# Routing over 32 masked logits, a gather of its own for the first pair of experts, and the last pair's gate and up products put ahead of the down product in front of it

## The chip, the cores and the metric

One NeuronCore of a Trainium2 chip runs the whole program in one launch. The metric is the device time of an execution in microseconds (us); the time before is the median of three runs, 1452.24 us (1451.04 to 1452.6). Matrix work runs on TensorE (PE), element-wise work on VectorE (DVE), ScalarE (ACT) and GpSimd (POOL); SyncE (SP) issues the transfers from the chip's memory (HBM).

## The reference, cut to what matters

Two transformer layers with a dense feed-forward part are followed by one block with two kinds of attention and a mixture of experts (MoE), and a last norm. 256 tokens of width 1024; 32 experts in 4 groups of 8; two experts a token, both from the token's best group. The part that the change touches:

```python
def hier_moe(h, w_group, b_group, w_router, b_router, w_e_gate, w_e_up, w_e_down):
    g_logits = hf @ w_group + b_group                       # 256 x 4
    g_probs, g_top = softmax(g_logits), argmax(g_logits)
    g_w = g_probs[g_top]
    e_logits = (hf @ w_router + b_router).reshape(-1, 4, 8)[:, g_top]   # 256 x 8
    e_w, e_idx = lax.top_k(softmax(e_logits), 2)
    e_w = e_w / e_w.sum()
    gates = one_hot(g_top * 8 + e_idx, 32) weighted by g_w * e_w        # 256 x 32
    for e in range(32):                                     # 1024 -> 512 -> 1024
        a = silu(hf @ w_e_gate[e]) * (hf @ w_e_up[e])
        out = out + gates[:, e:e+1] * (a @ w_e_down[e])
    return out

x = x + hier_moe(rmsnorm(x, g_ffn), ...)
return rmsnorm(x, g_final)
```

All arithmetic is in float32. The weights of the experts are 32 x 3 matrices of 2 MB, some 200 MB in all.

## The kernel before, in words

All weights come through one stream (`Stream`, lines 154 to 231): a list of units, most of them of 1 MB, in the order in which they are used, loaded by SP into slots of SBUF. `pump` issues the next unit as soon as a slot is free, `free` gives a slot back when the matmuls that read it have been written down. The slots come from tiles named raw, raw_left, raw_right, arena and arena_y, so a transfer into any of these from in_w_e_gate, in_w_e_up or in_w_e_down is a unit of the experts.

Up to the MoE a planner sets the order of the side work. From `route` on the order of each engine is the order of the code.

`route` (line 1955) makes the choice on DVE from the logits `lg` (two halves of 128 tokens, 4 group and 32 expert logits each). `top` finds the first maximum of a row as a one-hot: a maximum, a comparison, a product with a falling ramp, a maximum, a comparison. It runs on the 4 groups, then, after the 8 logits of the chosen group have been picked out with a product and a sum, twice on 8 logits. The one-hot of both experts is spread to 32 columns (`s32`), and two matmuls count the tokens in front of each token (`place`: which of an expert's CAP = 32 places it has). While DVE does this, PE runs WARM matmuls whose result nobody reads (`ident` by `x`, 512 columns; PE takes each float32 matmul in two passes, and the profile counts passes).

`side_batch` (line 2130) readies 8 experts (4 pairs) at a time: `places` writes the one-hot of token and place for them (2 x 256 columns, tile arena_y), `rows(k2)`, for k2 = 0 to 3, gathers the tokens into `xe` with 4 matmuls of 128 x 256 (two of the 8 blocks of the width), `scales` gathers the norm's factors, and two steps `back` make the gated transpose that scatters the results. These steps stand in a list (`todo`), from which `side` takes one or two between the steps of a pair.

`moe` (line 2309) goes through 16 pairs of experts (NQ). A pair q takes `emit_rows(q, 0)` and `emit_rows(q, 1)` (gate and up products; each reads 4 units of 1 MB, 16 matmuls, four at a time in four strips of 32 columns of PE's array: two experts, gate and up), `emit_act` (tanh on ACT, two steps on DVE), `emit_at` (four transposes and an ACT copy) and `emit_down` (4 units of 1 MB). After each second pair `emit_scatter` adds the results into four banks of PSUM, which also take `x`.

The order of the stream is pair by pair: 8 units of gate and up, 4 of down. The last pair's down comes in 8 units of 0.5 MB (`last_down`), the first four for output columns 0 to 511, the others for 512 to 1023. `last_norm` (line 2362) takes the last pair's down product in these two halves: matmuls, a copy of the 64 rows to SBUF (`Y`), two scatter matmuls, and for each 128 tokens a square with a sum (ACT) and the product with `g_final` (DVE). Then POOL makes the factor of the norm, ACT and DVE scale, and four transfers of 256 KB write the output. A branch (`If self.most > CAP`), for the case that an expert gets over 32 tokens, stands inside the last pair; it is not entered.

Of the kernel before, what the change touches and what calls it, by code (L numbers as in the profile page):

```python
# [13 lines left out]
P = 128  # L14
T = 256
D = 1024
# [34 lines left out]
WARM = 5  # L51
# [519 lines left out]
class Kernel:  # L571
# [992 lines left out]
    def plan2(self):  # L1564
# [32 lines left out]
        def last_down(q):  # L1597

            for c in range(2):
                for h in range(2):  # L1600
                    for e in (2 * q, 2 * q + 1):
                        src = self.A["w_e_down_2"][0][e][h * 256 : h * 256 + 256, c * 512 : c * 512 + 512]
                        self.exp_units[q].append(
                            self.st.add(512, 2, [(0, 512, src.rearrange("(p k) c -> p k c", p=P))], split=False)
                        )

        for q in range(NQ):
            rows(q)
            (down if q < NQ - 1 else last_down)(q)
# [250 lines left out]
    def mix2(self):  # L1860
# [44 lines left out]
        self.gp = self.small([P, 2, 4], "gp", bufs=1)  # L1905
        for h in range(2):
# [48 lines left out]
    def route(self):  # L1955
# [22 lines left out]
        def top(v, n, oh):  # L1978

            m = sc(f"top{n}{oh}", 1)  # L1980
            o = sc(f"oh{n}{oh}", n)
            t = sc(f"tt{n}", n)
            V.tensor_reduce(out=m, in_=v, axis=AX.X, op=ALU.max)
            V.tensor_tensor(out=t, in0=v, in1=bc(m, 2, n), op=ALU.is_equal)
            V.tensor_tensor(
                out=t, in0=t, in1=bc(self.tab(f"first{n}").unsqueeze(1), 2, n), op=ALU.mult
            )
            f = sc(f"tf{n}", 1)
# [5 lines left out]
        gm, go = top(gl, 4, "a")  # L1994
        el, e48 = sc("el", 8), sc("e48", 4, 8)
        V.tensor_tensor(
            out=e48,
            in0=lg[:, :, 4:36].rearrange("p t (g e) -> p t g e", g=4),
            in1=bc(go.unsqueeze(3), 2, 4, 8),
            op=ALU.mult,  # L2000
        )
        V.tensor_reduce(out=el, in_=e48.rearrange("p t g e -> p t e g"), axis=AX.X, op=ALU.add)
        m1, o1 = top(el, 8, "a")
        e2 = sc("e2", 8)
        V.scalar_tensor_tensor(out=e2, in0=o1, scalar=-BIG, in1=el, op0=ALU.mult, op1=ALU.add)
        m2, o2 = top(e2, 8, "b")
        s32, sel = sc("s32", 4, 8), sc("sel", 8)

        def spread(out, v):
            V.tensor_tensor(out=out, in0=bc(go.unsqueeze(3), 2, 4, 8), in1=bc(v.unsqueeze(2), 2, 4, 8), op=ALU.mult)  # L2010

        V.tensor_tensor(out=sel, in0=o1, in1=o2, op=ALU.add)
        spread(s32, sel)
        s32 = s32.rearrange("p t g e -> p t (g e)")
# [11 lines left out]
        self.gate = sc("g32", 4, 8)  # L2026

        def gates():
            den = sc("den", 1)
            V.tensor_reduce(out=gs, in_=ge, axis=AX.X, op=ALU.add)  # L2030
            V.scalar_tensor_tensor(out=den, in0=v, scalar=1.0, in1=gs, op0=ALU.add, op1=ALU.mult)
            V.reciprocal(out=den, in_=den)
            V.tensor_tensor(out=o2, in0=o2, in1=bc(v, 2, 8), op=ALU.mult)
            V.tensor_tensor(out=o1, in0=o1, in1=o2, op=ALU.add)
            V.tensor_tensor(out=o1, in0=o1, in1=bc(den, 2, 8), op=ALU.mult)
            spread(self.gate, o1)
            self.gate = self.gate.rearrange("p t g e -> p t (g e)")
# [92 lines left out]
    def side_batch(self, b):  # L2130
# [6 lines left out]
        def places():  # L2137
            for tb in range(2):
                nc.vector.tensor_tensor(
                    out=d[:, tb].rearrange("p (e s) -> p e s", e=8),  # L2140
                    in0=self.place[:, tb, e0 : e0 + 8].unsqueeze(2).to_broadcast([P, 8, CAP]),
                    in1=self.tab("iota").unsqueeze(1).to_broadcast([P, 8, CAP]),
                    op=ALU.is_equal,
                )
            self.xe[b] = self.room(NK, 8 * CAP)

        def rows(k2):
# [3 lines left out]
            for i in range(2):  # L2151
                k = k2 * 2 + i
                for tb in range(2):

                    c0 = (k // 4) * 512
                    self.mm(ps[:, i, :], self.x[:, tb, c0 + k % 4 : c0 + 512 : 4], d[:, tb, :], tb == 0, tb == 1)
            gain = lambda k: self.gp[:, k // 4, k % 4 : k % 4 + 1]
            k = k2 * 2
            nc.scalar.activation(out=xe[:, k, :], in_=ps[:, 0, :], func=AF.Copy, scale=gain(k))
            nc.vector.tensor_scalar(out=xe[:, k + 1, :], in0=ps[:, 1, :], scalar1=gain(k + 1), scalar2=None, op0=ALU.mult)  # L2160
# [35 lines left out]
        steps = [places] + [lambda k2=k2: rows(k2) for k2 in range(4)] + [scales]  # L2196
# [73 lines left out]
    def emit_at(self, th):  # L2270

        ps = self.ps(5)[:, 0:256]
        for k in range(4):

            c0 = (k // 2) * 256
            self.tr(ps[:, k * 64 : k * 64 + 64], th[0:64, c0 + k % 2 : c0 + 256 : 2])
# [32 lines left out]
    def moe(self):  # L2309
# [14 lines left out]
        for q in range(NQ):  # L2324
# [7 lines left out]
            if q == NQ - 1:  # L2332
                side(99)
# [3 lines left out]
            if q == NQ - 1:  # L2337
                with self.tc.If(self.most > CAP):
                    self.overflow()
                self.gfin = self.room(D)  # L2340
                nc.gpsimd.dma_start(out=self.gfin, in_=self.A["g_final_2"].unsqueeze(0).to_broadcast([P, D]))
# [11 lines left out]
            if q == NQ - 1:  # L2353
                break
# [5 lines left out]
        self.last_norm(at)  # L2360

    def last_norm(self, at):
# [3 lines left out]
        outs = [[self.room(512) for tb in range(2)] for c in range(2)]  # L2366
        for c in range(2):
            self.emit_down(NQ - 1, at, c)
            self.emit_scatter(NQ // 2 - 1, c)
            for tb in range(2):  # L2370
                ps = self.ps(c * 2 + tb)
                nc.scalar.activation(
                    out=self.ps(7), in_=ps, func=AF.Square, scale=D ** -0.5, accum_out=self.ssq[:, tb, c : c + 1]
                )
                V.tensor_tensor(out=outs[c][tb], in0=ps, in1=self.gfin[:, c * 512 : c * 512 + 512], op=ALU.mult)
        v = self.small([P, 2], "v")
        nc.gpsimd.tensor_tensor(out=v, in0=self.ssq[:, :, 0], in1=self.ssq[:, :, 1], op=ALU.add)
        nc.gpsimd.tensor_scalar(out=v, in0=v, scalar1=EPS, scalar2=None, op0=ALU.add)
        self.pow(self.rstd, v)
        for c in range(2):  # L2380
            for tb in range(2):
                o, r = outs[c][tb], self.rstd[:, tb : tb + 1]
                if c + tb == 0:
# [3 lines left out]
                (nc.sync if c else nc.scalar).dma_start(  # L2387
# [282 lines left out]
```

## Time and profile before

| | |
|---|---|
| median of 3 runs | 1452.24 us (1451.04 to 1452.6) |
| profiled execution | 1452.91 us, its span 1451.1 us |
| PE busy | 1311.3 us (90%), 8865 passes |
| DVE, ACT, POOL busy | 724.6, 559.8, 215.9 us |
| transfers | 360.21 MB, mean 248 GB/s |
| granted PE clock, mean | 0.953 of full |

The span is the time from the first to the last instruction that the profiler recorded. A row of a timeline has the start, the time taken, the engine and the line, the operation, what it writes and reads, and the shape. Line 258 is that of a helper that issues every instruction, so rows are told apart by their tiles. PE is the matmul itself, PEld the loading of its stationary operand, SPq the issue of a transfer on SP's queue. A matmul's row holds its way through the array too, so matmuls that follow each other overlap in the rows. In a row of windows the busy time and the count of each engine stand in the order PE, PEld, DVE, ACT, POOL, then the granted PE clock (1.00 is 2.4 GHz, 0.50 is 1.2 GHz), the busy share of the 16 transfer engines and what they moved.

### The profile page before, as it was taken

The numbers are of one execution on the slowest core, as the hardware profiler recorded it, in microseconds if no ns is written. First come the engines' busy times: TensorE is split into PE (matmuls) and PEld (weight loads), VectorE is DVE, ScalarE is ACT, GpSimd is POOL, SyncE is SP. The second block draws the span as 40 slices with busy tenths as digits, with TensorE's granted clock in tenths as the row PEclk, the third lists the DMA queues.
The fourth block names the chain that finished last, engine by engine and source line by source line (L and its number), as shares of the span: only waits on it lengthen the run. The fifth ranks groups of instructions, "written<-read, shape, count | busy, mean of one in ns | idle before, by whom it ended". The sixth has DMA issues, their size and how long they took to land.

```text
span 1451.1 us, 23004 instructions
## 1 busy us (share of the span) xinstructions
PE 1311.3 (90%) x8865; PEld 977.9 (67%) x8865; DVE 724.6 (50%) x1521; ACT 559.8 (39%) x1175; POOL 215.9 (15%) x345
## 2 busy tenths in 40 slices
PE   9989999999999999999999999998887777867665
PEld 8777999988777899988989899885332311412111
DVE  5586677765588677765676655563210200110001
ACT  5526555554536555545564546541110100100001
POOL 2154111101055011102442302010000000000000
PEclk9998999999999999999999999999989979988888
DMA  9651556555524465557435354688999999999995
GB/s 342 193 170 47 162 179 199 167 195 177 178 96 147 131 189 183 186 188 225 152 94 169 117 163 141 220 327 354 419 420 420 421 421 420 420 421 421 421 419 211
DMA packets 155076, 360.21 MB, mean 248 GB/s; under 512 B 8752, under 2 KB 98352, under 8 KB 130768
## 3 DMA queue, kind: packets, MB, share of 16 engines
q1 hardware_dynamic: 152928, 354.81, 66.8%
q0 software_dynamic: 1248, 3.11, 0.7%
q8 instruction: 71, 1.16, 0.3%
q10 hardware_dynamic: 784, 0.76, 0.2%
q14 instruction: 45, 0.37, 0.1%
HBM read 357.60 MB, written 1.05 MB: 247 GB/s over the span
## 4 chain that ended last, share of the span: by engine, by line
PE 41%; DMA 22%; DVE 3%; ACT 2%; POOL 1%; issue 1%; POOLq 0%; DVEq 0%; SPq 0%; ACTq 0%
PE psum L258 41%; DMA raw<-in_w_e_up_dram 8%; DMA raw_left<-in_w_e_down_dram 3%; DMA arena_y<-in_w_e_up_dram 3%; DMA raw<-in_w_e_down_dram 3%; DMA raw_right<-in_w_e_up_dram 3%; DMA raw_right<-in_w_e_down_dram 1%; DMA raw_left<-in_w_e_up_dram 1%; DVE arena L258 1%; ACT whi L258 1%; ACT arena L258 1%; DVE wlo L258 1%; POOL arena L258 1%; DVE arena_o L258 0%; ACT arena_o L258 0%
## 5 line engine op out<-in xcount | busy, mean ns | idle before, releaser
L258 DVE TENSOR_TENSOR wlo<-raw,whi 128x512 fp32r<-128x512 f32 (+3 forms) x552 | 397.2, 727 | 260.5 <-ACT whi L258 249.4
L258 ACT CAST whi<-raw 128x512 fp32r<-128x512 f32 (+3 forms) x552 | 332.8, 606 | 344.6 <-PE psum L258 274.4
L258 PE MATMUL psum<-h_hi,whi 128*128 128x256 f32 x1040 | 297.8, 286 | 3.0 <-ACT whi L258 3.0
L258 PE MATMUL psum<-h_lo,whi 128*128 128x256 f32 x1040 | 291.6, 280 | 0.1
L258 PE MATMUL psum<-h_hi,wlo 128*128 128x256 f32 x1040 | 290.2, 279 | 0.0
L258 PEld LDWEIGHTS psum<-h_hi,whi 128*128 128x128 f32 x1040 | 195.8, 188 | 10.1 <-issue 4.8
L258 PEld LDWEIGHTS psum<-h_lo,whi 128*128 128x128 f32 x1040 | 196.2, 189 | 0.9 <-issue 0.5
L258 PEld LDWEIGHTS psum<-h_hi,wlo 128*128 128x128 f32 x1040 | 196.0, 188 | 0.2 <-DVE wlo L258 0.2
L258 PE MATMUL psum<-raw,arena 128*32 128x512 f32 x608 | 164.0, 672 | 19.1 <-DMA raw<-in_w_e_up_dram 12.6
L258 PE MATMUL psum<-arena 64*128 64x128 f32 (+10 forms) x752 | 160.1, 418 | 21.6 <-DVE arena L258 8.2
L258 PE MATMUL psum<-whi,h_hi 128*128 128x256 f32 (+3 forms) x448 | 145.8, 325 | 1.4 <-ACT arena_o L258 1.1
L258 PE MATMUL psum<-whi,h_lo 128*128 128x256 f32 (+3 forms) x448 | 138.3, 309 | 0.0
L258 PE MATMUL psum<-wlo,h_hi 128*128 128x256 f32 (+3 forms) x448 | 138.3, 309 | 0.0
L258 PEld LDWEIGHTS psum<-arena 64*128 64x128 f32 (+4 forms) x752 | 73.1, 175 | 69.8 <-issue 23.7
L258 DVE SCALAR_TENSOR_TENSOR arena<-arena,psum 128x256 f32<-128x256 f32 (+2 forms) x36 | 17.8, 517 | 201.7 <-ACT arena L258 198.8
L258 PEld LDWEIGHTS psum<-raw,arena 128*32 128x32 f32 x608 | 34.4, 121 | 99.8 <-issue 60.3
L258 PE MATMUL psum<-raw_left,arena 128*32 128x512 f32 x400 | 81.2, 712 | 20.9 <-DMA raw_left<-in_w_e_gate_dram 14.8
L258 POOL TENSOR_TENSOR arena<-arena 128x512 f32<-128x512 f32 (+2 forms) x46 | 49.0, 1074 | 295.3 <-DVE arena L258 289.0
L258 PEld LDWEIGHTS psum<-whi,h_hi 128*128 128x128 f32 x448 | 85.3, 190 | 11.0 <-issue 4.4
L258 PEld LDWEIGHTS psum<-wlo,h_hi 128*128 128x128 f32 x448 | 85.4, 191 | 4.6 <-issue 1.4
L258 PEld LDWEIGHTS psum<-whi,h_lo 128*128 128x128 f32 x448 | 85.2, 190 | 4.5 <-DVE h_lo L258 0.2
L258 DVE COPY arena<-psum 128x384 f32<-128x384 f32 (+6 forms) x60 | 32.6, 543 | 108.0 <-ACT arena L258 95.7
(247 smaller groups left out, 1761.5 us busy)
## 6 DMA issues: line engine op xcount, KB each, us to landing
raw<-in_w_e_up_dram SPq DMA_DIRECT2D x32, 1024.0 KB, 19.8
raw<-in_w_in_dram SPq DMA_DIRECT2D x60, 512.0 KB, 4.9
raw<-in_w_e_gate_dram SPq DMA_DIRECT2D x24, 1024.0 KB, 19.8
raw<-in_w_gate_dram SPq DMA_DIRECT2D x44, 512.0 KB, 4.0
raw<-in_w_up_dram SPq DMA_DIRECT2D x44, 512.0 KB, 5.1
raw<-in_w_down_dram SPq DMA_DIRECT2D x20, 1024.0 KB, 5.2
raw_left<-in_w_e_gate_dram SPq DMA_DIRECT2D x20, 1024.0 KB, 19.9
raw<-in_w_e_down_dram SPq DMA_DIRECT2D x19, 1024.0 KB, 19.8
```

The costliest lines, as they stand in the source:

```text
L258: return f(*args, **kw)
```

## The change

**Routing.** The three parts of `el` go: instead of the product, the sum over the groups and a choice among 8, the logits of the other groups get -BIG (`top(..., others=True)` gives the one-hot of those that are not the first maximum), and both choices are made on 32 columns, with a ramp `first` of 32 that POOL writes in `mix2`. Two spreads from 8 to 32 columns go too. The one-hots and the scratch lie in a room of the arena that `gates` drops. WARM goes from 5 to 3.

**First pair.** For the first 8 experts, `places` and `rows` take columns c0 to c1: first those of pair 0 alone (64 columns), later, after the pair's second half, those of pairs 1 to 3 (192 columns).

**Last pair.** The stream takes the gate and up units of pair 15 ahead of the down units of pair 14, and `moe` does the same with `emit_rows` and `emit_act`; the branch and the load of `g_final` stand behind them. The last down comes in 512, 256 and 256 output columns, one unit an expert and piece, and `last_norm` has one round for each.

```diff
-WARM = 5
+WARM = 3
...
-            for c in range(2):
-                for h in range(2):
-                    for e in (2 * q, 2 * q + 1):
...
+            for c0, n in ((0, 512), (512, 256), (768, 256)):
+                for e in (2 * q, 2 * q + 1):
+                    src = self.A["w_e_down_2"][0][e][:, c0 : c0 + n].rearrange("(p k) c -> p k c", p=P)
+                    self.exp_units[q].append(self.st.add(n, 4, [(0, n, src)], split=False))
...
+        for q in range(NQ - 1):
             rows(q)
-            (down if q < NQ - 1 else last_down)(q)
+            if q == NQ - 2:
+                rows(NQ - 1)
+            down(q)
+        last_down(NQ - 1)
...
-            V.tensor_tensor(out=o, in0=t, in1=bc(f, 2, n), op=ALU.is_equal)
+            V.tensor_tensor(out=o, in0=t, in1=bc(f, 2, n), op=ALU.is_lt if others else ALU.is_equal)
...
-        V.tensor_reduce(out=el, in_=e48.rearrange("p t g e -> p t e g"), axis=AX.X, op=ALU.add)
-        m1, o1 = top(el, 8, "a")
...
+        V.scalar_tensor_tensor(
+            out=el.rearrange("p t (g e) -> p t g e", g=4),
+            in0=bc(no.unsqueeze(3), 2, 4, 8),
+            scalar=-BIG,
+            in1=lg[:, :, 4:36].rearrange("p t (g e) -> p t g e", g=4),
+            op0=ALU.mult,
+            op1=ALU.add,
         )
+        m1, _ = top(el, self.first, 32, "a", (o1, t))
+        V.scalar_tensor_tensor(out=e2, in0=o1, scalar=-2.0 * BIG, in1=el, op0=ALU.mult, op1=ALU.add)
+        m2, _ = top(e2, self.first, 32, "b", (o2, t))
+        V.tensor_tensor(out=s32, in0=o1, in1=o2, op=ALU.add)
...
+            one, rest = slice(0, 2 * CAP), slice(2 * CAP, 8 * CAP)
+            steps = [lambda: places(0, 2)] + [lambda k2=k2: rows(k2, one) for k2 in range(4)]
+            steps += [lambda: (places(2, 8), scales())] + [lambda k2=k2: rows(k2, rest) for k2 in range(4)]
...
+            if q == NQ - 2:
+                side(99)
+
+                for h in range(2):
+                    self.emit_rows(NQ - 1, h)
+                last = self.emit_act(NQ - 1)
+                self.ar.drop(self.xe.pop(b))
+                with self.tc.If(self.most > CAP):
+                    self.overflow()
+                self.gfin = self.room(D)
+                nc.gpsimd.dma_start(out=self.gfin, in_=self.A["g_final_2"].unsqueeze(0).to_broadcast([P, D]))
             self.emit_down(q, at, None)
...
+        self.last_norm(self.emit_at(last, True))
...
+        for n, (c0, w) in enumerate(((0, 512), (512, 256), (768, 256))):
+            c, cs = c0 // 512, slice(c0 % 512, c0 % 512 + w)
+            r0 = 0 if c else 64
+            for x in range(2):
+                for k in range(4):
+                    o = r0 + x * CAP
+                    wk = self.st.slot(units[2 * n + x])[:, k, :]
+                    self.mm(y[o : o + CAP, cs], at[:, k, x * CAP : x * CAP + CAP], wk, k == 0, k == 3)
+            nc.scalar.copy(out=self.Y[r0 : r0 + 64, c, cs], in_=y[r0 : r0 + 64, cs])
             for tb in range(2):
...
+                self.mm(ps, gt[:, (q // 2) % 2, c, tb * P : tb * P + P], self.Y[:, c, cs], False, True)
                 nc.scalar.activation(
+                    out=self.ps(7)[:, 0:w], in_=ps, func=AF.Square, scale=D ** -0.5, accum_out=ssq[:, tb, n : n + 1]
...
+        for tb in range(2):
+            r, vt = self.rstd[:, tb : tb + 1], v[:, tb : tb + 1]
+            (V if tb else nc.gpsimd).tensor_tensor(out=vt, in0=ssq[:, tb, 2:3], in1=vt, op=ALU.add)
+            self.pow(r, vt)
```

On PE, from the last matmuls of the logits to the first matmuls of the experts (x by tab_67 are the WARM matmuls, arena_y by x is the gather, raw by arena the experts):

```order
 L258 MATMUL psum<-wr,arena 128x36 x8
-L258 MATMUL psum<-x,tab_67 128x512 x5
-L258 MATMUL psum<-s_9426,tab_67 128x64
-L258 MATMUL psum<-s_9426,ones 128x32
-L258 MATMUL psum<-arena_y,x 128x256 x8
+L258 MATMUL psum<-x,tab_67 128x512 x3
+L258 MATMUL psum<-s_9420,tab_67 128x64
+L258 MATMUL psum<-s_9420,ones 128x32
+L258 MATMUL psum<-arena_y,x 128x64 x8
 L258 MATMUL psum<-raw_83,arena 32x512
 L258 MATMUL psum<-raw_81,arena 32x512
```

Two WARM matmuls go, and the gather in front of the first expert matmul has 64 columns instead of 256.

On SP, the end of the stream before (a row is a transfer; w_e_gate and w_e_up are the units of emit_rows):

```order
L258 DMA raw_left_9376<-in_w_e_down_dram 128x2048
L258 DMA raw_left_9377<-in_w_e_gate_dram 128x2048
...
L258 DMA raw_85<-in_w_e_up_dram 128x2048
L258 DMA raw_80<-in_w_e_down_dram 128x2x512
...
L258 DMA raw_82<-in_w_e_down_dram 128x2x512
L258 DMA arena_y<-in_w_e_down_dram 128x2x512 x2
```

and now:

```order
L258 DMA raw_83<-in_w_e_up_dram 128x2048
L258 DMA raw_84<-in_w_e_down_dram 128x2048
...
L258 DMA raw_85<-in_w_e_down_dram 128x2048
L258 DMA raw_80<-in_w_e_down_dram 128x4x512
L258 DMA raw_right_9172<-in_w_e_down_dram 128x4x512
L258 DMA raw_right_9173<-in_w_e_down_dram 128x4x256
...
L258 DMA raw_82<-in_w_e_down_dram 128x4x256
```

The four down units of pair 14 stood in front of the eight gate and up units of pair 15 and stand behind them now; the last four units have rows of 256 columns.

On PE, the last down product before, from the transposes on (tab_67 by arena; arena by arena with 128x512 are the scatters):

```order
L258 MATMUL psum<-tab_67,arena 128x64 x4
L258 MATMUL psum<-raw_80,arena 32x512
L258 MATMUL psum<-raw_right_9172,arena 32x512
L258 MATMUL psum<-raw_80,arena 32x512
L258 MATMUL psum<-raw_right_9172,arena 32x512
...
L258 MATMUL psum<-arena 128x512 x2
...
L258 MATMUL psum<-arena_y,arena 32x512 x4
L258 MATMUL psum<-arena 128x512 x2
```

and now:

```order
L258 MATMUL psum<-tab_67,arena 128x64 x4
L258 MATMUL psum<-raw_80,arena 32x512 x4
L258 MATMUL psum<-raw_right_9172,arena 32x512 x4
L258 MATMUL psum<-arena 128x512 x2
L258 MATMUL psum<-raw_right_9173,arena 32x256 x4
L258 MATMUL psum<-raw_right_9174,arena 32x256 x4
L258 MATMUL psum<-arena 128x256 x2
L258 MATMUL psum<-arena 32x256 x4
L258 MATMUL psum<-raw_82,arena 32x256 x4
L258 MATMUL psum<-arena 128x256 x2
```

Where the two experts took turns (raw_80, raw_right_9172), one expert's four matmuls now stand together and the other's behind them.

## Rows read from the trace of the kernel before

**Rows 1.** Windows: around the stop of the stream, and the steady stretch.
```profile
996.00:1001.50 5.50, 5.50 (x41) 2.64 (x41) 0.66 (x2) 0.47 (x1) 0.00 (x0) 1.00 0.06 25
1001.50:1010.00 8.50, 7.71 (x62) 4.76 (x61) 1.12 (x3) 1.61 (x4) 0.00 (x0) 1.00 1.01 394
1300.00:1400.00 100.00, 70.98 (x350) 17.54 (x346) 7.77 (x11) 5.81 (x11) 0.00 (x0) 0.85 1.01 421
```

**Rows 2.** Chain of waits that ended last: start, time, what (merged).
```profile
1091.38 19.82 DMA raw_right<-in_w_e_up_dram
...
1401.41 19.94 DMA raw<-in_w_e_up_dram
...
1421.40 3.63 PE psum L258 x26
...
1428.57 5.35 PE psum L258 x16
...
1434.58 5.57 PE psum L258 x20
...
1440.90 2.00 PE psum L258 x4
```

**Rows 3.** Timeline from the logits to the first transfer after the stop.
```profile
983.71 1.98 PE L258 MATMUL psum<-wr,arena 128*128 128x36 f32 x16 [0.34 <-DVE arena L258]
...
985.52 6.23 PE L258 MATMUL psum<-x,tab 128*128 128x512 f32 x10
...
987.23 0.22 DVE L258 TENSOR_TENSOR e<-lg,oh4a 128x64 f32<-128x64 f32 x1
...
987.49 0.26 DVE L258 TENSOR_REDUCE el<-e 128x16 f32<-128x64 f32 x1
...
990.28 0.22 DVE L258 TENSOR_TENSOR s<-oh4a,sel 128x64 f32<-128x64 f32 x1
...
991.59 0.33 PE L258 MATMUL psum<-s,tab 128*128 128x64 f32 x2
...
992.16 0.23 DVE L258 SCALAR_TENSOR_TENSOR place<-psum,s 128x64 f32<-128x64 f32 x1 [1.50 <-PE psum L258]
992.42 0.76 DVE L258 TENSOR_TENSOR arena_y<-place,tab 128x256 f32<-128x256 f32 x2
...
992.90 4.11 PE L258 MATMUL psum<-arena_y,x 128*128 128x256 f32 x16 [0.78 <-DVE arena_y L258]
...
996.94 3.64 PE L258 MATMUL psum<-raw,arena 128*32 128x512 f32 x32
...
1000.59 1.28 SPq L258 DMA_DIRECT2D raw<-in_w_e_down_dram  x3
```

**Rows 4.** Timeline of SP: the third issue after the stop.
```profile
1016.59 0.33 SPq L258 DMA_DIRECT2D raw_right<-in_w_e_up_dram  x1
```

**Rows 5.** Windows: PE's granted clock after small matmuls, and in the last down.
```profile
982.00:985.50 3.50, 2.78 (x24) 2.54 (x24) 1.62 (x3) 1.17 (x4) 1.09 (x3) 1.00 1.03 428
985.50:989.00 3.50, 3.50 (x7) 1.43 (x7) 2.76 (x15) 0.00 (x0) 0.00 (x0) 0.52 1.01 419
...
1429.40:1432.70 3.30, 3.30 (x10) 0.76 (x8) 0.00 (x0) 0.00 (x0) 0.00 (x0) 0.50 0.69 257
```

**Rows 6.** Timeline of the last 20 us: copy, norm factor, scaling.
```profile
1433.94 0.58 ACT L258 COPY arena<-psum 64x512 f32<-64x512 f32 x1 [5.42 <-PE psum L258]
...
1444.36 0.72 POOL L258 TENSOR_TENSOR rstd<-v,tab 128x2 f32<-128x2 f32 x1
1445.12 0.72 ACT L258 ACTIVATE arena<-arena,rstd 128x512 f32<-128x512 f32 x1 [1.45 <-POOL rstd L258]
1445.12 1.28 DVE L258 TENSOR_SCALAR arena<-arena,rstd 128x512 f32<-128x512 f32 x3 [0.72 <-POOL rstd L258]
```

**Rows 7.** Timeline of PE: one expert matmul alone, in two passes.
```profile
1386.94 1.04 PE L258 MATMUL psum<-raw_right,arena 128*32 128x512 f32 x2
```

**Rows 8.** Windows: full transfer engines on rows of 1 KB (input projection) and 2 KB.
```profile
665.00:670.00 5.00, 5.00 (x24) 4.09 (x23) 2.79 (x5) 2.11 (x4) 0.00 (x0) 1.00 1.03 303
...
1422.00:1428.00 6.00, 3.64 (x30) 1.16 (x18) 1.43 (x2) 0.68 (x1) 0.00 (x0) 1.00 1.04 391
```

More of the change, by code (lines that the diff above doesn't have):

```diff
@@ L1905, in mix2 @@
         self.gp = self.small([P, 2, 4], "gp", bufs=1)
+        self.first = self.small([P, 32], "first", bufs=1)
+        nc.gpsimd.tensor_scalar(out=self.first, in0=self.tab("iota"), scalar1=-1.0, scalar2=33.0, op0=ALU.mult, op1=ALU.add)
         for h in range(2):
@@ L1976, in bc, with top @@
             return a.to_broadcast([P, *shape])
[L1978 to L1982, printed above, removed]
+        def top(v, first, n, oh, room, others=False):
+            m, f = sc(f"top{n}{oh}", 1), sc(f"tf{n}", 1)
+            o, t = room
             V.tensor_reduce(out=m, in_=v, axis=AX.X, op=ALU.max)
             V.tensor_tensor(out=t, in0=v, in1=bc(m, 2, n), op=ALU.is_equal)
[L1985 to L1988, printed above, removed]
+            V.tensor_tensor(out=t, in0=t, in1=bc(first.unsqueeze(1), 2, n), op=ALU.mult)
@@ L2025, in route @@
         nc.scalar.activation(out=v, in_=v, func=AF.Exp)
-        self.gate = sc("g32", 4, 8)
+        self.gate = sc("g32", 32)
         def gates():
@@ L2194, in back @@
             self.ar.drop(dg)
-        steps = [places] + [lambda k2=k2: rows(k2) for k2 in range(4)] + [scales]
+        if b:
+            steps = [places] + [lambda k2=k2: rows(k2) for k2 in range(4)] + [scales]
+        else:
+            one, rest = slice(0, 2 * CAP), slice(2 * CAP, 8 * CAP)
+            steps = [lambda: places(0, 2)] + [lambda k2=k2: rows(k2, one) for k2 in range(4)]
+            steps += [lambda: (places(2, 8), scales())] + [lambda k2=k2: rows(k2, rest) for k2 in range(4)]
         return steps, [lambda pr=pr: back(pr) for pr in range(2)]
@@ L2268, in emit_act, with emit_at @@
         return th
-    def emit_at(self, th):
+    def emit_at(self, th, last=False):
         ps = self.ps(5)[:, 0:256]
@@ L2322, in side @@
                     todo.pop(0)()
-        for q in range(NQ):
+        for q in range(NQ - 1):
             b = q // 4
@@ L2365, in last_norm @@
         V = nc.vector
[L2366 to L2369, printed above, removed]
+        q = NQ - 1
+        units = self.exp_units[q][8:]
+        outs = [self.room(D) for tb in range(2)]
+        ssq = self.small([P, 2, 3], "ssq3", bufs=1)
+        v = self.small([P, 2], "v")
+        y = self.ps(6)
+        gt = self.gt[(q // 2) // 2]
+        for n, (c0, w) in enumerate(((0, 512), (512, 256), (768, 256))):
[7 more added lines that the diff above has]
+            nc.scalar.copy(out=self.Y[r0 : r0 + 64, c, cs], in_=y[r0 : r0 + 64, cs])
@@ L2374, in last_norm @@
                 )
[L2375 to L2380, printed above, removed]
-            for tb in range(2):
-                o, r = outs[c][tb], self.rstd[:, tb : tb + 1]
-                if c + tb == 0:
+            for tb in range(2):
+                ps = self.ps(c * 2 + tb)[:, cs]
+                V.tensor_tensor(out=outs[tb][:, c0 : c0 + w], in0=ps, in1=self.gfin[:, c0 : c0 + w], op=ALU.mult)
@@ new lines, in last_norm @@
+            if n == 1:
+                nc.gpsimd.tensor_tensor(out=v, in0=ssq[:, :, 0], in1=ssq[:, :, 1], op=ALU.add)
+                nc.gpsimd.tensor_scalar(out=v, in0=v, scalar1=EPS, scalar2=None, op0=ALU.add)
+        for tb in range(2):
+            r, vt = self.rstd[:, tb : tb + 1], v[:, tb : tb + 1]
+            (V if tb else nc.gpsimd).tensor_tensor(out=vt, in0=ssq[:, tb, 2:3], in1=vt, op=ALU.add)
+            self.pow(r, vt)
+            for c in range(2):
+                o = outs[tb][:, c * 512 : c * 512 + 512]
+                if c:
```

70 lines of the change are left out of this document (22 added, 48 removed).

## Prediction

> **What bounds the kernel now.** I read the slices of the span first: from slice 28 on the transfer engines are full. The windows [rows 1] say how full: 421 GB/s over 1300 to 1400 us, at a busy share of 1.01, and PE at 71%. So from the experts' start the time is that of the stream, and a 1 MB unit costs 1.05 MB / 421 = 2.49 us. The chain of waits [rows 2] agrees: from 1091 to 1421 us it is transfer on transfer. What the change can win lies where the stream isn't the bound: before it runs full, and after its last gate and up unit.
>
> The first place is a stop. From 996.0 to 1001.5 us the engines are 6% busy, then 394 GB/s follow at once [rows 1]: all slots were filled, none was free. The timeline [rows 3] shows what frees the first: routing on DVE, the count and the gather on PE, the first sixteen expert matmuls (996.94 to 1000.58), then SP's issue at 1000.59. As the stream never stops again, each microsecond that this issue comes sooner is one less in the span.
>
> The second place is the end. The last gate and up unit lands at 1421.4 [rows 2]. From there PE and its helpers run: activation, a down product in two halves with a scatter each, norm, output, 29.7 us to the end of the span at 1451.1. The last 4 MB of the stream lie beside it.
>
> **The start, step by step, at PE's full clock.** DVE took 3.27 us from `e` (987.23) to the end of `s` (990.50), 15 instructions. Now there are 13, on 64 columns (two halves of 32): 7 products, comparisons and sums at 0.22 (rows `e`, `s`), 2 of the kind with a scalar at 0.23 (row `place`), 4 maxima at 0.26 (row `el`, which reads 64 columns too), and 0.04 between starts (`e` to `el` is 0.26 for 0.22): 3.04 + 0.52 = 3.56. `s` ends 0.3 us later, at 990.8 [rows 3].
>
> That cost is covered by a wait of before: `s` lay ready at 990.50, but PE took it up at 991.59, behind ten WARM passes that held it for 6.23 us from 985.52. Four go, at 0.43 each (the pace of 512 columns at full clock, below), 1.7 us: WARM ends at about 990.0, and `s` starts at 990.85, 0.74 sooner. `place` follows 0.57 later as before, at 991.42; the first of two comparisons now has 64 columns (0.22) where it had 256 (0.76 for two), so the gather starts at 992.0, not 992.90 [rows 3].
>
> The gather in front of the first expert matmul had 16 passes of 256 columns, 4.11 us. No row shows 64 columns; 16 passes with 36 columns and the same stationary size took 1.98, so it lies between 1.98 and 4.11. I take 2.0, near the row of 36, because there the loading of 128 columns sets the pace (0.12 a pass). The experts start at 994.0, not 996.94, and with the same 3.64 us SP issues at 997.65: **2.9 us less**, between 0.9 (gather at 4.11) and 2.9.
>
> What is added: the gather of pairs 1 to 3, 32 passes of 192 columns at some 0.2 (between 0.12 and 0.26 by the rows of 36 and 256), 6.4 us, so that the gathers take 10.4 in place of 8.2 us. 24 of these passes, 4.8 us, now stand in front of pair 0's down product, which also frees slots. It is covered: the second issue comes 2.9 + 2.1 = 5 us sooner than before, and the third issue came at 1016.59 [rows 4] while 8 units issued since 1000.59 last 20 us, to 1021; 4.9 us of slack bear the 2.7 us that are not beside the activation. If that slack were gone, the stop would only move.
>
> **The end, on the clock of before (the 2.9 us not yet taken off).** Pair 15's last gate and up unit lands four units sooner, 1421.4 - 4 x 2.49 = 1411.4, its activation and the branch lie beside the 10 us of pair 14's down units, which land by 1421.4. Their last half takes PE 1.8 (half of 16 matmuls in 3.64), the transposes and copy 1.2: 1424.4. The first last-down unit lands 1.05 MB / 391 = 2.7 us behind, at 1424.1 [rows 8]. The last product starts at 1424.4; before it started at 1428.57 [rows 2].
>
> But it takes longer. A float32 matmul of 512 columns is two passes, 1.04 us alone [rows 7]; 16 of them in four strips take 3.64 us [rows 3], eight turns of 0.43 and a run-out of 0.2. Before, the two experts took turns in two strips and shared each turn. Now one expert's four matmuls, all into the same strip, stand in front of the other's, so only the seam overlaps: 15 turns, 6.4 us for 512 columns, 3.2 for 256.
>
> The Trainium skill, "TensorE: Matmul & The Clock Gate", section "Part 3: Packing small matmuls — row/col tiling", says the same against the change: loads of the stationary operand may be pulled ahead, but matmuls start and end strictly in program order. By that rule the sum is as here; without it the time would be the third rival's.
>
> So: first piece 1430.8; copy 0.58 and 0.1 of handing over [rows 6], 1431.5; scatter 2.0 [rows 2], 1433.5; second piece 3.2, copy 0.5, scatter 1.0 (half the columns), 1438.2; third the same, 1442.9. Before, PE ended at 1442.9 too [rows 2]. From there the last scaling ended 3.5 us later (1445.12 + 1.28 [rows 6]), and 4.7 us after that the span. Now the squares are half as wide (-0.3), the constant is added beforehand (-0.3), the second factor queues behind the first on POOL (+0.7), and each engine scales 512 columns once behind it (0.72 for 1.28, -0.6): 3.0. **End 1450.6, 0.5 us less.** Rows of 1 KB move slower than those of 2 KB, 303 against 391 GB/s [rows 8], 1.6 us on the last 2 MB, but the last unit then lands at 1433.7, long before PE asks for it, so I cost it at nothing.
>
> **PE's clock.** Both sums assume 2.4 GHz. In 982.0 to 985.5 PE's rows show 2.78 us busy with transposes and passes of 36 columns at full clock; the next 3.5 us were granted 0.52. The last down before ran 3.3 us at 0.50 [rows 5], a loss of 1.65 us. The change makes the start sparser: fewer WARM passes, two short waits and a gather of short passes. And PE waits longer in front of the last down. One more stretch like these, in either place, is what I expect: +1.65.
>
> **Sum.** -2.9 - 0.5 + 1.65 = -1.75 us. The profiled execution took 1452.91 (span 1451.1 and 1.8 around it), so 1451.2 on its own scale; the median of the runs is 0.7 below it, so 1450.5.
>
> **Rivals.**
> 1. *Full clock in both places*: -3.4, 1448.8. For it: WARM still ends under 1 us before `s`. Against: the drop behind the logits' small passes.
> 2. *The clock falls at the start and stays low through gather and experts, and once more in the last down*: slower. The gather takes 4.0, the experts 7.3: 992.0 to 1003.3, and the stop becomes 2.7 us longer than before; with 1.65 lost at the end -3.4 + 2.0 + 3.65 + 1.65 = +3.9, 1456.1. It is slower from 3.4 us of lost PE work on, measurably so from 6.3. For it: a gather of 64 columns resembles the 36 that went ahead of the drop [rows 5]; against: 3.64 us of dense experts at its end.
> 3. *PE starts the second expert's matmuls beside the first's*: pieces of 3.4 and 1.7; then the last unit's landing at 1433.7 binds, and 1.7 + 0.5 + 1.0 + 3.0 + 4.7 end at 1444.6: -6.5 - 2.9 = -9.4, 1442.8. Against: the order of the rows.
> 4. *The start wins nothing*, because the later gathers starve the stream in turn: -0.5, 1451.7. For it: PE is on the chain up to 1091 [rows 2]. Against: the slack above.
>
> **How the numbers follow.** The forecast with one low stretch has 42% (1449 to 1452.5 by itself), rival 1 25%, rival 2 16%, rival 3 6%, rival 4 7%, 4% for what I don't see. A measurement here tells 0.2%, 2.9 us, from no change. Faster by more: 0.10 of the forecast, 0.19 of rival 1, rival 3, 0.01: 0.36. Slower by more: 0.13 of rival 2, 0.03 of the others: 0.16. The rest, 0.48, is no change. The range goes from 1446.5 (rival 1 with some overlap in the strips) to 1455 (most of rival 2).
>
> **What would show it.** The stop: transfer share near nothing from about 997 to 998.6, first issue after it near 997.7 (999.3 with a low stretch; 1003 for rival 2). The gather: 16 passes in about 2.0. `s` taken up within 0.1 us of its end. The last down: one expert's four matmuls in a row, 15 turns of 0.43 in the first piece, PE's end near 1440, later by a low stretch. I am wrong if transfers stop again between 1005 and 1400, if the second expert's rows start among the first's, or if the last landing ends the chain.

## The result and the profile after

The changed kernel takes 1460.39 us (median of 4 runs, 1457.74 to 1464.08) against 1452.42 before: ratio 1.006, 95% interval 1.0048 to 1.0072. That is 7 to 10.5 us slower, outside the predicted range. The profiled execution took 1457.74 us with a span of 1456.0. Its logits start 1.05 us later than before (984.76 for 983.71), though the program up to there has the same instructions, so I count from the logits: 467.4 us to the end of the span before, 471.2 now. The profiled execution is the quickest of the four (the slowest took 1464.08), so its rows show 4.9 us of the 8.0 between the medians, 3.8 of them behind the logits.

Windows of the changed kernel (busy time of PE, PEld, DVE, ACT, POOL; PEclk, DMA share, GB/s), the stop first, as in [rows 1], then the clock, as in [rows 5]:

```profile
996.00:1001.50 5.50, 5.50 (x37) 1.79 (x36) 0.28 (x1) 0.31 (x1) 0.00 (x0) 0.72 0.18 72
1028.00:1030.00 2.00, 2.00 (x23) 0.63 (x25) 0.00 (x0) 0.59 (x1) 0.00 (x0) 1.00 0.73 209
1300.00:1400.00 100.00, 69.53 (x346) 17.32 (x346) 7.61 (x11) 5.62 (x10) 0.00 (x0) 0.85 1.01 420
...
996.00:998.00 2.00, 2.00 (x12) 1.07 (x15) 0.28 (x1) 0.31 (x1) 0.00 (x0) 0.50 0.49 197
...
1422.70:1429.00 6.30, 3.72 (x20) 1.15 (x24) 0.00 (x0) 0.00 (x0) 0.61 (x1) 0.50 1.05 375
```

The stop is still there, and at 1028 the stream falls a second time, to 209 GB/s for two microseconds. PE's granted clock is 0.50 over the first experts (996 to 998) and again in pair 14's down product (1422.7 to 1429). The timeline of the start answers [rows 3] and [rows 4]:

```profile
984.76 1.98 PE L258 MATMUL psum<-wr,arena 128*128 128x36 f32 x16 [0.34 <-DVE arena L258]
986.57 2.82 PE L258 MATMUL psum<-x,tab 128*128 128x512 f32 x6
...
991.37 0.22 DVE L258 TENSOR_TENSOR s<-arena 128x64 f32<-128x64 f32 x1
...
991.65 0.43 PE L258 MATMUL psum<-s,tab 128*128 128x64 f32 x2 [2.26 <-DVE s L258]
...
992.86 4.00 PE L258 MATMUL psum<-arena_y,x 128*128 128x64 f32 x16 [0.58 <-DVE arena_y L258]
...
996.79 4.73 PE L258 MATMUL psum<-raw,arena 128*32 128x512 f32 x32
...
1001.54 1.28 SPq L258 DMA_DIRECT2D raw<-in_w_e_down_dram  x3
...
1010.67 0.33 SPq L258 DMA_DIRECT2D raw<-in_w_e_up_dram  x1
...
1020.31 0.33 SPq L258 DMA_DIRECT2D raw_right<-in_w_e_up_dram  x1
```

PE takes up `s` 0.06 us after its end, 0.99 us sooner after the logits than before. But 16 passes of 64 columns take 4.00 us, where 256 columns took 4.11, and the experts 4.73 for 3.64. The first issue comes 16.78 us after the logits (16.88 before), the third 35.55 (32.88).

The timeline of the end answers [rows 6] and the last links of [rows 2]:

```profile
1417.04 1.02 PE L258 MATMUL psum<-raw,arena 128*32 128x512 f32 x2
...
1419.53 0.75 DVE L258 SCALAR_TENSOR_TENSOR arena<-arena,r2e,psum 64x512 f32<-64x512 f32 x1
...
1425.28 5.52 PE L258 MATMUL psum<-raw,arena 128*32 128x512 f32 x32 [7.22 <-DVEq L2356]
1425.83 0.61 POOL L258 DMA_DIRECT2D arena<-in_g_final_dram  x1 [440.22 <-DVEq L2356]
...
1432.28 2.31 PE L258 MATMUL psum<-raw,arena 128*32 128x512 f32 x5 [0.85 <-ACT arena L258]
1433.99 0.62 PE L258 MATMUL psum<-raw_right,arena 128*32 128x512 f32 x1
1434.42 0.59 PE L258 MATMUL psum<-raw,arena 128*32 128x512 f32 x1
...
1435.31 2.31 PE L258 MATMUL psum<-raw_right,arena 128*32 128x512 f32 x5
...
1440.20 2.81 PE L258 MATMUL psum<-raw_right,arena 128*32 128x256 f32 x16
...
1444.52 1.00 PEld L258 LDWEIGHTS psum<-arena 128*32 128x32 f32 x6 [0.33 <-issue]
```

PE is done with pair 15's rows at 1418.06, DVE with their activation at 1420.28. Then PE stands until 1425.28 and POOL with it; both name DVE's sequencer (DVEq) at line 2356, the branch. In the kernel before PE lost 0.52 us at its branch (line 2338):

```profile
1417.66 1.02 PE L258 MATMUL psum<-raw,arena 128*32 128x512 f32 x2 [0.52 <-PEq L2338]
```

Pair 14's down product follows at the low clock, 5.52 us, so the last pair's down product starts at 1432.28.

### The profile page after: what moved, and what is told of

The parts are those of the page before. It is cut to its first block, busy times and chain, and to the rows that moved or that the text cites. A ratio compares the mean times of both kernels' runs of the same rounds, so it can differ in the third digit from the quotient of the medians.

```text
span 1456.0 us, 23120 instructions
## 1 busy us (share of the span) xinstructions
PE 1318.0 (91%) x8913; PEld 985.0 (68%) x8913; DVE 727.2 (50%) x1525; ACT 563.1 (39%) x1186; POOL 216.1 (15%) x348
## 3 DMA queue, kind: packets, MB, share of 16 engines
HBM read 357.60 MB, written 1.05 MB: 246 GB/s over the span
## 5 line engine op out<-in xcount | busy, mean ns | idle before, releaser
L258 PE MATMUL psum<-raw,arena 128*32 128x512 f32 (+1 forms) x616 | 164.3, 700 | 25.4 <-DMA raw<-in_w_e_up_dram 11.0
L258 PE MATMUL psum<-arena 64*128 64x128 f32 (+10 forms) x760 | 155.1, 404 | 20.1 <-DVE arena L258 7.4
L258 ACT ACTIVATE arena<-psum,rhe 64x512 f32<-64x512 f32 x16 | 10.9, 682 | 191.2 <-PE psum L258 191.1
```

Of the source, the lines that this page charges most:

```text
L258: return f(*args, **kw)
```

## The experiments

Each ran on one chip with the kernel before beside it, 5 to 12 times; times are medians, ratios are to before, with the 95% interval in brackets. A second measure is the span behind the logits in the one profiled execution, since the stretch ahead of them varies (981.2 to 986.9 over the profiles, by 5.2 us between e10 and e14, whose buffers lie at the same places).

### The halves, and the branch

`e1_head_only`: before, with the functions of the start (routing, gather, `WARM = 3`) from after. 

> The kernel before with the change of the start alone (routing on 32 columns, WARM 3, the gather split into 64 and 192 columns); the end as before. Theory A (a gather pass is paced by the loading of its strided stationary block, 0.24 us whatever its columns): the first gather stays near 4 us, the gathers of the first eight experts take 16 us of PE instead of 8, the first issue comes no sooner and the stream stops a second time near 1028 us: 1453.5 to 1456. Rival C (it is PE's clock alone, low over the first experts): slower than before by 1 to 2 us with one stop, no second one. If the start had won what was forecast: 1449 to 1451.

1454.06 us, 1.0016 (1.0002 to 1.0031): slower by some 2 us. Not the gain forecast for the start.

`e2_tail_only`: before, with the functions of the end from after. 

> The kernel before with the change of the end alone (last pair ahead, branch behind its activation, three pieces); the start as before. Theory B (all wait at the branch, which DVE passes 5 us after pair 15's activation): PE stands still for about 5 us between pair 15's gate and up products and pair 14's down, and the time is 1453 to 1457. Rival (the loss of the changed kernel comes from the start alone): 1450 to 1452.

1457.57, 1.0038 (1.0028 to 1.0049): slower by 5.7 us, the place of the buffers included (below).

`e3_no_branch`: the changed kernel, without the overflow's work:

```diff
-                with self.tc.If(self.most > CAP):
-                    self.overflow()
```

> The changed kernel without the branch for overfull experts (that part of the computation is left out). Theory B: PE starts pair 14's down when its units land, near 1420, not 1425; the last down starts 4 to 5 us sooner, the time falls by 4 to 5 us against the changed kernel, to 1453 to 1457. Rival D (PE waited for units of the stream that landed late, the branch is only what the row names): within 1 us of the changed kernel.

1448.74, 0.9978 (0.9968 to 0.9988): 11.6 us below the changed kernel, where 4 to 5 were expected from a stand of 5 us. Something else had changed with it.

`e4_early_branch`: the branch and the load of the final gains between the two halves of pair 15's rows:

```diff
-                for h in range(2):
-                    self.emit_rows(NQ - 1, h)
+                self.emit_rows(NQ - 1, 0)
+                with self.tc.If(self.most > CAP):
+                    self.overflow()
...
+                self.emit_rows(NQ - 1, 1)
```

> The changed kernel with the branch and the load of g_final moved up between the two halves of pair 15's gate and up products, where DVE and ACT have been idle for long. Theory B: as without the branch, 4 to 5 us less than the changed kernel. Rival B2 (the branch costs its 5 us wherever it stands): 0 to 1 us less.

1455.59, 1.0023 (1.0013 to 1.0033): 4.8 of the 11.6 us.

### The place of the buffers

The compiled programs show what e3 had changed. The new three-column sum of squares is one more small tile (`e2` has it too), and tiles follow one another in each partition: the stream's buffers of the left side start at byte 36576, where before they started at 36544; without the branch's tiles at 36480. To a multiple of 256 they are off by 224, 192 and 128 bytes. The next runs change only that, by tiles that nothing uses:

```diff
         self.gp = self.small([P, 2, 4], "gp", bufs=1)
+        self.pad = self.small([P, 8], "pad", bufs=1)          # 32 bytes; 16: 64, 24: 96
+        self.open("rpad", "right", [("rpad", [P, 56], F32)])  # e12, e13, e15 to e17, first in body: 224
```

`e5_changed_pad32`: 

> The changed kernel with one more small tile of 32 bytes that nothing reads. In the program as compiled the change itself (its sum of squares has three columns) moved all stream buffers by 32 bytes, from 36544 in the kernel before (a multiple of 64) to 36576 (not one); the pad moves them on to 36608 (a multiple of 128). Theory P (the place of the buffers costs time): the logits come 1 to 4 us sooner than in the changed kernel's kind of profile (before: 983.7, end change alone: 986.9), the steady stream goes from 420 to 423 or 424 GB/s as in the kernel without the branch (whose buffers lie at 36480, a multiple of 128), and the time falls by 5 to 9 us against the changed kernel, to 1451 to 1455. Theory B (the branch alone costs the 11 us between the changed kernel and the one without it): no difference beyond 1 us, 1459 to 1461.

1454.89, 1.0020 (1.0010 to 1.0029): 5.5 us back.

`e6_before_pad32`: 

> The kernel before with the same pad of 32 bytes, and nothing else: its stream buffers then lie where the changed kernel has them (36576). Theory P: slower than before by 2 to 5 us (1454 to 1457), with the drift of about 1 us near 300 us and near 640 to 690 us of the span that the changed kernel shows. Theory B: within 1 us of the kernel before (1451 to 1453).

1454.65, 1.0016 (1.0007 to 1.0026): an unused tile makes the kernel before slower by 2.7 us.

`e7_before_pad64`: 

> The kernel before with a pad of 64 bytes: buffers from a multiple of 64 to a multiple of 128 (36608). Theory P with 128 bytes as the step: stream at 423 to 424 GB/s instead of 421, 2 to 3 us faster than before (1449 to 1450). Theory P with 64 bytes as the step, and theory B: no difference (1451 to 1453).

1451.04, 0.9988 (0.9979 to 0.9997).

`e8_no_branch_pad96`: 

> The changed kernel without its branch (so without the overflow's work) and with a pad of 96 bytes, so that its buffers lie exactly where the changed kernel has them (36576): against the changed kernel only the branch and its body are missing. Theory P: 5 to 7 us slower than without the pad, 1454 to 1456, and the branch itself is worth the 4 to 6 us left to the changed kernel. Theory B: as without the pad, 1448 to 1450.

1456.98, 1.0030 (1.0019 to 1.0041): most of e3's gain was the place. At the changed kernel's own places the branch is worth 3.4 us.

`e12_before_pad64_right`: 

> The kernel before with the 64 bytes of pad and, at the other end of the memory, a second pad of 224 bytes, so that all stream buffers start at multiples of 256: with 64 bytes alone, those of the right side stay at 183264, 199648 and 207840, which are 32 bytes short of one. Theory P (a transfer into a buffer off such a multiple takes longer): the rest of the stream's buffers gains as the first did, 425 to 426 or 427 GB/s in the steady stretch, 1 to 2 us less than 1451.0. By the Trainium skill, page DMA: Bandwidth & Descriptors, section How a descriptor splits into AXI transactions, a descriptor that starts off a multiple of 256 bytes begins with a transaction of which a part is unused, so by it the gain lasts up to a multiple of 256. Rival (only the buffers of the left side matter, or what moved the time was something else that lies there): 1450.5 to 1451.5.

1448.05, 0.9971 (0.9960 to 0.9982). With two unused tiles the kernel before is 4.4 us faster than it was in the same runs. The window of the full stream, of e5 and of e12:

```profile
1300.00:1400.00 100.00, 69.92 (x354) 17.18 (x352) 7.77 (x11) 6.00 (x11) 0.00 (x0) 0.88 1.01 424
```
```profile
1300.00:1400.00 100.00, 71.42 (x372) 18.07 (x364) 8.46 (x12) 6.58 (x12) 0.00 (x0) 0.89 1.01 427
```

The rate orders with the offset of the left side. Over 1100 to 1400 us of each profile it is 420 GB/s at 224 bytes, 421 at 192, 423 at 128 (e3 alone), 425 at 0, and 426 to 427 with the right side at 0 too. Over the 430 us of the stream 420 for 425 is an estimated 5 us. Behind the logits the profiles agree: 462.4 us in e7 for 467.4 before, 467.4 in e5 for 471.2 in the changed kernel. The Trainium skill, "DMA: Bandwidth & Descriptors", section "How a descriptor splits into AXI transactions", says that a descriptor that does not start at a multiple of 256 bytes begins with a transaction part of whose bytes are unused; the order of the rates agrees. Why 32 bytes cost 2.7 us from 192 to 224, where the rate hardly differs, stays open: in e6 the logits start 2.1 us later than before (985.82), the span behind them is 0.4 shorter (467.0), and the variation ahead of the logits is as large.

`e13_changed_all_placed`: the changed kernel with both pads. 

> The changed kernel with the pad of 32 bytes on the left side and that of 224 on the right: all stream buffers at multiples of 256, as in the kernel before with 64 and 224 bytes (1448.05). Theory (place, start and branch add up): 427 GB/s steady, 1451 to 1453, that is 3 to 5 us slower than the kernel before at the same places, of which 4.3 are the branch and 1.9 the start, less the 1.4 that the end gains. Rival (the whole loss was the place, as the branch and the start measured before are bound to the buffers off a multiple): 1448 to 1449.

1455.61, 1.0017 (1.0008 to 1.0026): 427 GB/s, and no gain over e5, outside both ranges expected. Why the faster stream gives nothing here is not shown; it stays so with the branch out of the way (e17 below, 1451.13, for e10's 1450.64 with the left side placed alone). Against e12 the change itself costs 7.6 us here (6.0 behind the logits), against e7 at e5's places 3.9 (5.0), against e6 at its own 5.7 (4.2).

### The branch

`e10_early_pad32`: e4 with the pad. 

> The changed kernel with the pad of 32 bytes, and the branch and the load of the gains for the final norm between the two halves of pair 15's rows, where the matmuls stand in the kernel before around its branch. Theory: from the last weight's landing to the end it takes 16.6 us (as in the kernel with the early branch at the old place of the buffers) instead of 19.5, so 3 us less than the padded changed kernel: 1451 to 1453. Rival (the branch costs its time wherever it stands, by the landing itself): within 1 us of 1454.9.

1450.64, 0.9985 (0.9976 to 0.9994): 4.3 us for the branch's place. PE still waits at it, but there pair 15's next unit lands only 1 us later:

```profile
1407.66 2.92 PE L258 MATMUL psum<-raw_left,arena 128*32 128x512 f32 x6 [2.79 <-PEq L2354]
1408.15 0.61 POOL L258 DMA_DIRECT2D arena<-in_g_final_dram  x1 [420.90 <-PEq L2354]
1408.65 0.19 PEld L258 LDWEIGHTS psum<-raw_left,arena 128*32 128x32 f32 x4 [0.89 <-DMA raw_left<-in_w_e_gate_dram]
```

`e17_short_body`: e13 with one expert in the overflow instead of 32:

```diff
-        for e in range(NE):
+        for e in range(1):
```

> The changed kernel with all stream buffers at multiples of 256 (1455.61), its branch where the change puts it, and in the branch's body the work of one expert instead of all 32 (17 instructions on VectorE instead of 358, 82 on TensorE instead of 2004), so that the overflow of the other 31 is left out. Theory J (the engine goes on late because the code behind the body has to be brought in): TensorE's 7.0 us of waiting for VectorE at the branch shrink to 0 to 2, and the time falls by 4 to 7 us, to 1448.5 to 1451.5. Rival M (branching and meeting cost the 5 to 7 us by themselves, whatever the length): the wait stays above 5 us and the time within 1 us of 1455.6.

1451.13, 0.9988 (0.9979 to 0.9997): 4.5 us less, with the branch in the same place. The end of the activation and the next product, of e13 and of e17:

```profile
1416.96 0.75 DVE L258 SCALAR_TENSOR_TENSOR arena<-arena,r2e,psum 64x512 f32<-64x512 f32 x1
...
1422.54 6.52 PE L258 MATMUL psum<-raw,arena 128*32 128x512 f32 x32 [7.04 <-DVEq L2357]
```
```profile
1416.01 0.75 DVE L258 SCALAR_TENSOR_TENSOR arena<-arena,r2e,psum 64x512 f32<-64x512 f32 x1
1416.92 4.28 PE L258 MATMUL psum<-raw,arena 128*32 128x512 f32 x32 [2.38 <-DVEq L2357]
```

From DVE's last activation to PE it is 4.83 us with the long body (5.00 in the changed kernel) and 0.16 with the short one: what is jumped over sets the price. The edit shortens the body on all engines at once, so it does not tell whose length counts. The transfer view of the changed kernel, 1420.3 to 1425.2 us (packets, MB, share of 16 engines), has what comes in meanwhile; with the short body no such packet falls between 1414 and 1427. That the engines wait for these packets fits theory J, but no run shows it by itself.

```profile
q8 instruction: 1, 0.02, 1.4%
q14 instruction: 2, 0.02, 0.9%
```

### The start

`e9_contig_pad32`: e5, but the gather of the first eight experts loads neighbouring columns:

```diff
-                    self.mm(ps[:, i, c], self.x[:, tb, c0 + k % 4 : c0 + 512 : 4], d[:, tb, c], tb == 0, tb == 1)
+                    xs = self.x[:, tb, k * P : k * P + P] if b == 0 else self.x[:, tb, c0 + k % 4 : c0 + 512 : 4]
+                    self.mm(ps[:, i, c], xs, d[:, tb, c], tb == 0, tb == 1)
```

> The changed kernel with the pad of 32 bytes, where the gather for the first eight experts loads 128 neighbouring columns of the tokens (8 stretches of 128) instead of every fourth of 512; it gathers other columns than the reference wants, so only its time is read. Theory S (a load of every fourth column takes 0.24 us, of neighbouring columns 0.12, and this load paces the gather): the first 16 passes take 2.0 us instead of 4.0, the second 16 (192 columns each, now paced by the columns) 2.5 to 3.3 instead of 4.1, the first issue after the logits comes 2 to 4 us sooner than in the padded changed kernel, and the time falls by 2 to 4 us from 1454.9, to 1451 to 1453. Rival C (the clock paces the start): the passes take half the time, but the matmuls of the first pair at the low clock take it back, and the time falls by less than 1 us.

1452.45, 1.0006 (0.9995 to 1.0016): 2.4 us less than e5 by the medians; the runs of the two overlap (1450.03 to 1457.28, 1451.74 to 1457.73). Its two gathers of the first pair:

```profile
994.17 2.86 PE L258 MATMUL psum<-arena_y,x 128*128 128x64 f32 x16 [0.57 <-DVE arena_y L258]
...
1002.98 2.00 PE L258 MATMUL psum<-arena_y,x 128*128 128x64 f32 x16
```

The second is the 2.0 us of the prediction to the digit, at a granted clock of 1.00; the first ran at 0.78 on the mean of 994 to 996. The other columns, 192 a pass, took 2.87 instead of 4.05. The first issue came no sooner, against theory S: 17.00 us behind the logits for e5's 16.86, because the first experts took 6.08 us at the low clock (0.50 from 996 to 1001). The gain shows behind it, in the third issue: 30.31 for 35.63. Over all profiles the third issue comes 34.5 to 35.6 us behind the logits with the new start and its strided loads, 31.6 to 33.4 with the old one, at whatever places. So the strided loads in their larger number are what delays it.

`e14_early_pad32_warm5`: e10 with `WARM = 5`. 

> The changed kernel with 32 bytes of pad and the early branch (1450.64), with five idle matmul groups behind the logits instead of three, as the kernel before has them. Theory S (the start costs by its strided loads, 16 passes at 0.25 us): the gather waits for the longer idle work by up to 0.7 us, so 1450.6 to 1451.5. Rival C (the clock): the clock stays at 1.00 to the first issue, which comes 1.5 us sooner after the logits than at 0.74 (16.8 instead of 18.4), so 1448.5 to 1449.5.

1450.69, 0.9986 (0.9978 to 0.9995): the same. Its first issue came 16.65 us after the logits instead of 17.60, its second 25.78 instead of 25.04: given back at once. The clock did not stay at 1.00, as rival C had it (0.64 from 991 to 994, and 4.61 us for the first experts), so what a full clock would be worth is not tested.

`e11_end_early_pad32`: e10 with the start of the kernel before. 

> The start of the kernel before, the changed end with the early branch, and the pad (buffers at 36608, as in the kernel before with 64 bytes of pad). Theory: the start alone is what keeps the padded changed kernel with the early branch slow, by 1.5 to 4 us (0.3 to 1.3 MB fewer landed 50 us after the logits); the end with its branch out of the way gains 1.4 us behind the last landing and loses up to 1.1 in front of it by its rows of 1 KB. So 1449.5 to 1451.5, against 1451.0 for the kernel before with 64 bytes of pad. Rival (the start is worth nothing): as the run before it, 1451 to 1453.

1448.77, 0.9976 (0.9965 to 0.9986): against e10 the new start costs 1.9 us by the medians. The runs overlap widely (1446.37 to 1452.25 here, 1447.58 to 1452.74 in e10), and behind the logits the profiles differ by 0.5. `e1` gives 2.2 for the start, just clear of the noise.

### Without branch, place and start in the way

`e15_end_early_all_placed`: e11 with both pads. 

> The start of the kernel before, the changed end with the early branch (1448.77 with 32 bytes of pad), and all stream buffers at multiples of 256. Theory: the places of the right side are worth what they were in the kernel before (1451.04 to 1448.05), so 1445.5 to 1446.5. Rival (the two gains overlap): 1447.5 to 1449.

1447.75, 0.9971 (0.9961 to 0.9981). By the medians 1 us below e11, in the rival's range, and 0.3 below e12, whose end is the old one; behind the logits 459.4 for e12's 462.0.

`e16_end_interleaved`: as e15, experts taking turns and the next piece's product ahead of this piece's spreading:

```diff
-            for x in range(2):
-                for k in range(4):
+            for k in range(4):
+                for x in range(2):
...
+        product(0)
+        for n in range(3):
+            if n < 2:
+                product(n + 1)
+            spread(n)
```

> As the run before it, with the last pair's product in another order: its two experts take turns matmul by matmul, and the product of the next piece of columns stands ahead of the spreading of this piece, which waits for a copy on ScalarE. Theory (the chain behind the last landing is serial work of TensorE, 12.5 us from landing to its last matmul in the changed kernel): 2 to 4 us less behind the last landing, 1442 to 1444. Rival (the last piece's landing sets the end, and only what follows it counts: one product of 2.8 us at best halved): 1 to 1.5 us less, 1444 to 1445.5.

1446.90, 0.9963 (0.9950 to 0.9976), 5.5 us under before and 13.5 under the changed kernel; against e15 0.9, under what either side expected and within the spread of the runs. The second piece now takes 1.92 us instead of 2.81:

```profile
1426.17 1.92 PE L258 MATMUL psum<-raw_right,arena 128*32 128x256 f32 x16 [0.67 <-ACT arena L258]
```

## Why the prediction was wrong

**The branch, costed at nothing: the largest step of the sum that failed.** The sum put "its activation and the branch" beside pair 14's down units. Their transfers did lie beside it; PE's work did not. DVE reaches the branch last, because the activation stands in front of it, and PE goes on 5.0 us after DVE's last step. Before, PE lost 0.5 at its branch. Price 4.3 us by e10, 4.5 by e17.

**A gain at the start of 2.9: failed; some 2 us lost (1.9 by e11, 2.2 by e1).** WARM and `s` came as worked out (0.99 sooner for 0.74, maxima 0.22 for 0.26). The gather gave 0.1 instead of 2.1, and the low clock over the first experts took 1.1 back, so the first issue came 0.1 us sooner. The gather was priced by the row of 36 columns, which loads neighbouring columns at 0.12 a pass. The gather loads every fourth column, 0.25 a pass for 64, 192 or 256 columns alike. The rows that said so were in the trace of before, the loads of the logits and of its gather in the timeline of PEld:

```profile
983.71 1.86 PEld L258 LDWEIGHTS psum<-wr,arena 128*128 128x128 f32 x16 [0.58 <-DVE arena L258]
...
992.89 3.81 PEld L258 LDWEIGHTS psum<-arena_y,x 128*128 128x128 f32 x16 [0.89 <-DVE arena_y L258]
```

So no pass became cheaper by fewer columns, and the gathers of the first eight experts took 16 us of PE instead of 8.2, not the 10.4 forecast. The 4.9 us of slack did not bear that: the third issue came 2.7 us later after the logits, and the stream fell to half again at 1028. Rival 4 was right that the later gathers starve the stream; it had the start win nothing, not lose.

**The place of the buffers: not in the sum at all.** The diff was read for instructions, and a tile of a few bytes has none. 2.7 us by e6, up to 5.5 by e5; no term of the sum and no rival had it.

**The end, forecast at -0.5: not settled.** The last pair's down product was to start at 1424.4 and started at 1432.28, behind the branch. With the branch early and the old start the changed end is 2.3 us below e7 (e11) and 0.3 below e12 (e15) by the medians, neither clear of the noise; behind the logits it is 1.3 longer and 2.6 shorter. From the start of that product to the end of the span it took 23.7 us for the 26.2 forecast (22.5 before). Two terms inside were off. The first piece took 5.35 us, not 6.4, since the second expert's passes began beside the first's last four: rival 3 in small. Of the first's eight passes three (from the row at 1434.42 on) start after the second's first (1433.99), so the strict order that the sum leaned on does not hold here. The second piece took 2.81 for 3.2. The 1 KB rows did no harm that binds: the stream is done by 1436.5 us, and the last piece's product began at 1444.5.

**The clock.** The low stretch in the last down product of before [rows 5] is gone; two came instead. The first experts lost 1.1 us (4.73 for 3.64), and pair 14's down 1.9 (5.52 for the same 3.64), behind the stand at the branch: together 3.0, less the 1.65 no longer lost: a net 1.35 for the 1.65 forecast. That it comes near is luck: two stretches came and one went, where one more was costed. WARM 5 brings nothing (e14), but the clock fell there too, so what the start's clock costs by itself stays open.

**Sum.** Place 2.7 (e6), branch 4.3 (e10), start 1.9 (e11), end -2.3 (e11 against e7): 6.6 of the 8.0 measured. Place and branch are clear of the noise; the sizes of start and end are not. The prices also depend on where they are measured: the place counts 2.7 from 192 bytes to 224 on the kernel before (e6) and 5.5 from 224 to 0 on the changed one (e5), the branch 3.4 (e8) to 4.8 (e4). How the rest divides stays open.

## What to carry to other kernels

Price a matmul's pass by its stationary load in the layout that it has, and look for that row before the one with the fitting column count. Look for a place for a conditional branch where its last engine arrives early, and cost the engines' wait there; here it was 4.83 us with a long body and 0.16 with a short one. When a change adds or drops a tile, compare where the stream's buffers lie, to a multiple of 256 bytes, before reading a few microseconds as the change's effect, and pad both kernels alike for the comparison.

## What the runs showed of the hardware

- Stream into buffers whose left side starts 224, 192, 128 or 0 bytes past a multiple of 256: 420, 421, 423 and 425 GB/s with the same transfers; with the right side at a multiple too, 426 to 427.
- A stationary load of 128 columns: 0.12 us from neighbouring columns, 0.24 from every fourth.
- A branch not taken over 358 instructions of DVE and 2004 of PE: 4.83 us until PE goes on; over 17 and 82: 0.16.
- Matmuls of a later instruction in another strip start while three passes of earlier ones are still to come.
